# Expert weights with consecutive rows per partition, both output halves per down tile, and 32 copies of a relative bias

## The chip, the cores and the metric

The kernel runs on one core of a Trainium2 chip. The metric is the time of one execution on the device in microseconds, measured on the chip; the median of several executions counts.

## What is computed

A sequence of 256 tokens of width 1024 passes through two blocks of two layers each. A layer has a mixer (attention or a recurrence) and a mixture of experts (MoE) with 16 experts. All is float32. The change touches the MoE of the second block and, in its second layer, the reading of a relative bias that an attention mixer adds to its scores. Cut to that:

```python
D_MODEL, SEQ, DEPTH = 1024, 256, 2
MOE_EXPERTS, MOE_TOPK, MOE_FF = 16, 2, 512

def hier_moe(x, w_group, b_group, w_router, b_router, w_gate, w_up, w_down):
    t = x.reshape(-1, D)
    ...                                   # combine: weight of each expert for each token, two of 16 not zero
    y = jnp.zeros_like(t)
    for e in range(MOE_EXPERTS):          # w_gate[e], w_up[e]: (1024, 512); w_down[e]: (512, 1024)
        hdn = jax.nn.silu(t @ w_gate[e]) * (t @ w_up[e])
        y = y + combine[:, e:e + 1] * (hdn @ w_down[e])
    return y.reshape(B, S, D)

def second_block(x, ...):
    h = x
    for layer in range(DEPTH):
        if layer < N_A_LAYERS:
            mix = gla_mixer(h, ...)
        else:                             # scores get rel_table[rel_bucket(kpos - qpos)] as bias
            mix = diff_attention(h, ..., k1, k2, v, rel_table, lambda_init)
        h = layer_norm(DEEPNORM_ALPHA * h + mix, ln_g[layer, 0], ln_b[layer, 0])
        ffn = hier_moe(h, ..., moe_w_gate[layer], moe_w_up[layer], moe_w_down[layer])
        h = layer_norm(DEEPNORM_ALPHA * h + ffn, ln_g[layer, 1], ln_b[layer, 1])
        if layer == N_A_LAYERS - 1:
            k1, k2, v = shared_kv(h, kv_w)
    return h
```

In the first block the experts have an inner width of 256, in the second of 512.

## The kernel before

The four MoE layers are called moe10, moe11 (first block) and moe20, moe21 (second block); one function `moe` builds all of them. `F` is the inner width and `NF = F // 128` is 2 in the first block and 4 in the second. Tokens are gathered for the experts: every expert takes up to 64 tokens, and experts are worked on in eight **pairs** `pi`, so that the two experts of a pair fill the 128 columns of TensorE, expert `j` the columns `64 * j` and on. Two pairs make a group of four experts, for which `gather` fetches the tokens by matmuls with a one-hot matrix `oh` (tile `pg`, from `z` split in a high part `zh` and a low part `zl`).

For each pair there are these steps. `up(pi)` computes gate and up into two PSUM tiles `gu`, by 64 instructions over eight weight tiles of 1 MB, and takes silu of the gate part into `sa` (L794, ScalarE). `act(pi)` multiplies the up part, the combine weight `cr` and `sa` (L830, VectorE), and transposes the result by four matmuls into `pat` (L833), which VectorE copies back (L834). `down(pi)` multiplies by four down tiles of 1 MB: a tile is one half `h` of the output (512 of 1024 columns) and one half `fh` of the inner width, for both experts, and it is loaded by two DMAs of 512 KB, each of rows of 2 KB. When one half `h` of `y` is complete, ScalarE copies it rounded to `yh` (L860), VectorE makes the remainder `yl` (L861), and `spread` multiplies both by the one-hot matrix `st` to bring the rows back to their tokens (tile `sc`, recorded at L334, a helper for all split matmuls). `land` adds `sc` to the running `X` (L892, VectorE). Then the other half follows. `pst` (L820) is a transposition that makes `st`.

The loop runs `up(pi + 1)`, `down(pi)`, `act(pi + 1)` and so on; a scheduler orders the instructions of each engine. After pair 4 all engines read a counter and branch around an overflow path that does not run here (L905, L907). Weights come by `wload` and `fetch` on SP's queue (L193) into 19 slots in rotation; before the layer begins, a `plan` already loads the first 22 tiles. Gate and up tiles are read by `kview`: partition p gets row p, p + 128 and so on, four rows of 2 KB for each half of the 1024 rows. For this `z` stands in its natural order: chunk k of 128 columns is contraction step k.

The relative bias is prepared by `bias_task` while moe11's weights are already arriving. It writes the table `fsb` (8 heads, 384 values) 128 times over into a scratch array `fd` in HBM (L1542, on ScalarE's queue), so that partition p can later read its own copy shifted by p, with a row pitch of 383 (L1783, tile `vb`, two DMAs on ScalarE's queue, one for four heads each). `vb` is read there at the end of moe20, when its buffer comes free.

## Time and profile before

| | |
|---|---|
| median of 3 runs | 1602.59 us (1598.65 to 1603.44) |
| the profiled execution | 1602.16 us, of which the span is 1600.4 us |
| TensorE busy | 92% of the span |
| VectorE, ScalarE, GpSimd busy | 54%, 27%, 8% |
| mean DMA rate over the span | 288 GB/s |

A row of the timeline is a run of equal instructions on one engine: start and length in us, engine, line, operation, the tile written and those read, and in brackets the idle time ahead of it with what ended it. PE is TensorE, DVE is VectorE, ACT ScalarE, POOL GpSimd; "SPq" and "ACTq" are the queues of SP and ScalarE, from which DMAs are issued. One down or gate/up matmul of the program's order is two instructions in the profile.

### The profile page before, as it was taken

To read this page: it belongs to the slowest core of one execution; us is meant where nothing else is said; L and a number is where in the kernel's file an instruction comes from. 1 tells how busy PE (TensorE), PEld (TensorE's weight loads), DVE (VectorE), ACT (ScalarE), POOL (GpSimd) and SP (SyncE) were. 2 spreads that over 40 slices of the span, in tenths; PEclk is the share of its full clock that TensorE was granted. 3 is DMA by queue.
4 is the path that set the end of the run, shared out by engine and by line. 5 is a ranking of instruction groups with operands and counts; after the bars stand their busy time and mean duration, and the time that the engine had idled before them with its cause. 6 is when DMAs were issued, how large, how long until landed. Compare 5 with 4: busy or idle time off the path is not lost. (4 is left out here: it accounts for less than half of the span.)

```text
span 1600.4 us, 22811 instructions
## 1 busy us (share of the span) xinstructions
PE 1470.0 (92%) x9124; PEld 969.4 (61%) x9124; DVE 869.0 (54%) x1686; ACT 432.8 (27%) x733; POOL 129.2 (8%) x140
## 2 busy tenths in 40 slices
PE   4999987998889999889989999999998999999895
PEld 3879987443478999734448895443337988434331
DVE  3689998343678879823464574231127776212214
ACT  1454331211235434111125331110103652101000
POOL 0200002000121000300011001000003002000001
PEclk9999999999979999889999999999999999999998
DMA  9978799995855769799887487999999966999993
GB/s 301 365 249 273 259 303 324 353 302 198 268 174 173 242 232 337 167 363 359 292 263 214 133 290 267 386 387 353 381 334 288 298 195 244 341 386 387 346 386 124
DMA packets 324371, 461.69 MB, mean 288 GB/s; under 512 B 20077, under 2 KB 178285, under 8 KB 324258
## 3 DMA queue, kind: packets, MB, share of 16 engines
q1 hardware_dynamic: 308720, 446.34, 81.5%
q10 hardware_dynamic: 15538, 13.81, 3.5%
q8 instruction: 76, 1.25, 0.3%
q14 instruction: 37, 0.30, 0.1%
HBM read 456.43 MB, written 3.67 MB: 287 GB/s over the span
## 5 line engine op out<-in xcount | busy, mean ns | idle before, releaser
L786 PE MATMUL gu<-w,xg 128*64 128x512 f32 x1536 | 369.2, 597 | 0.0
L786 PEld LDWEIGHTS gu<-w,xg 128*64 128x64 f32 x1536 | 110.8, 137 | 209.1 <-issue 202.7
L356 DVE TENSOR_TENSOR wlo<-w,whi 128x2048 fp32r<-128x2048 f32 (+2 forms) x92 | 183.3, 1994 | 44.9 <-ACT whi L346 44.2
L850 PE MATMUL y<-w,sa 128*64 128x512 f32 x768 | 195.6, 607 | 4.4 <-DMA w<-in_w_exp_down_dram 4.4
L346 ACT ACTIVATE whi<-w 128x2048 fp32r<-128x2048 f32 (+2 forms) x92 | 157.9, 1726 | 151.4 <-PE acc L427 111.6
L850 PEld LDWEIGHTS y<-w,sa 128*64 128x64 f32 x768 | 55.0, 138 | 106.0 <-issue 97.7
L830 DVE SCALAR_TENSOR_TENSOR sa<-gu,cr,sa 128x256 f32<-128x256 f32 (+1 forms) x32 | 19.7, 615 | 163.6 <-PE gu L786 136.4
L334 PE MATMUL sc<-yy,st 128*128 128x512 f32 x256 | 88.8, 436 | 18.1 <-ACT yy L860 14.3
L522 DVE SCALAR_TENSOR_TENSOR adac<-w,ce,adac 128x512 f32<-128x512 f32 x140 | 104.7, 748 | 1.2
L427 PE MATMUL acc<-hl,whi 128*128 128x256 f32 x608 | 93.3, 286 | 0.0
L427 PE MATMUL acc<-hh,whi 128*128 128x256 f32 x608 | 90.4, 289 | 1.6 <-ACT whi L346 1.6
L892 DVE TENSOR_TENSOR x<-x,sc 128x512 f32<-128x512 f32 x112 | 74.3, 683 | 30.4 <-PE sc L334 30.3
L427 PE MATMUL acc<-hh,wlo 128*128 128x256 f32 x608 | 85.9, 281 | 0.0
L334 PE MATMUL pg<-oh,zh 128*128 128x256 f32 x256 | 73.8, 319 | 13.1 <-DVEq L907 7.3
L334 PEld LDWEIGHTS sc<-yy,st 128*128 128x128 f32 x256 | 42.0, 188 | 70.7 <-ACT yy L860 36.0
L427 PEld LDWEIGHTS acc<-hh,whi 128*128 128x128 f32 x608 | 78.4, 190 | 6.8 <-issue 4.1
L427 PE MATMUL acc<-whi,hh 128*128 128x256 f32 x416 | 70.9, 303 | 12.2 <-ACT hh L1240 8.9
L427 PEld LDWEIGHTS acc<-hl,whi 128*128 128x128 f32 x608 | 79.6, 189 | 3.7 <-issue 3.2
L427 PEld LDWEIGHTS acc<-hh,wlo 128*128 128x128 f32 x608 | 77.3, 188 | 1.0 <-issue 0.8
L334 PEld LDWEIGHTS pg<-oh,zh 128*128 128x128 f32 x256 | 55.4, 218 | 27.8 <-issue 15.0
L334 PE MATMUL pg<-oh,zl 128*128 128x256 f32 x256 | 71.2, 308 | 0.9 <-issue 0.9
L860 ACT ACTIVATE yy<-y 128x512 fp32r<-128x512 f32 x32 | 19.1, 597 | 192.2 <-PE y L850 192.2
(376 smaller groups left out, 2107.8 us busy)
## 6 DMA issues: line engine op xcount, KB each, us to landing
w<-in_moe_w_gate_dram SPq DMA_DIRECT2D x64, 1024.0 KB, 12.1
w<-in_moe_w_up_dram SPq DMA_DIRECT2D x64, 1024.0 KB, 13.8
w<-in_moe_w_down_dram SPq DMA_DIRECT2D x128, 512.0 KB, 11.6
w<-in_w_ada_dram SPq DMA_DIRECT2D x47, 1024.0 KB, 7.2
w<-in_w_in_dram SPq DMA_DIRECT2D x40, 1024.0 KB, 5.6
w<-in_w_exp_gate_dram SPq DMA_DIRECT2D x64, 512.0 KB, 9.5
w<-in_w_exp_up_dram SPq DMA_DIRECT2D x64, 512.0 KB, 8.8
w<-in_w_exp_down_dram SPq DMA_DIRECT2D x64, 512.0 KB, 8.9
```

Source lines behind the costliest of these rows:

```text
L334: PE.matmul(dst, l, r, start=(i == 0), stop=(i == n - 1), skip_group_check=True)
L346: S.activation(hi[:, k0:k0 + n], w, AF.Copy)
L356: eng.tensor_tensor(lo[:, k0 + x:k0 + y], w[:, x:y], hi[:, k0 + x:k0 + y].bitcast(F32), op=OP.subtract)
L427: PE.matmul(dst, l, r, start=(start and i == 0), stop=(i == n - 1), skip_group_check=True)
L522: V.scalar_tensor_tensor(acc, ws[k // 4][:, k % 4], ce[:, k:k + 1], acc, op0=OP.mult, op1=OP.add)
L786: PE.matmul(gu[64 * j:64 * j + 64, :], xg[:, 4 * kh + k, (2 * pr + j) * CAP:(2 * pr + j + 1) * CAP], ws[j][:, k, :], start=(kh == 0 and k ...
L830: V.scalar_tensor_tensor(sg, u, cr, sg, op0=OP.mult, op1=OP.mult)
L850: PE.matmul(y[64 * j:64 * j + 64, :], aT[:, f, 64 * j:64 * j + 64], w[:, j, k, :], start=(f == 0), stop=(f == NF - 1), tile_position=(0, 6 ...
L860: S.activation(yh[:, hs], src, AF.Copy)
L892: V.tensor_tensor(X[:, tt, hs], X[:, tt, hs], sc, op=OP.add)
```

## The change

The block-2 gate and up tiles are now read by `rview`: partition p gets the rows 8p to 8p + 7, of which a tile holds four, so 8 KB lie together in HBM. To match, `zh` and `zl` are written in the order (k c) from a source in the order (c k). The inner width is permuted in the same way: silu writes `sa` in the order (k c), the product in `act` reads the up part `u` from PSUM with a step of 16 bytes, and a down tile gives partition p the rows 4p to 4p + 3, of which it holds two, 8 KB together. A down tile now belongs to one expert `j` and one `fh`, holds both output halves, and is one DMA of 1 MB. Both halves of `y` are accumulated side by side, and they are copied and spread when all is done. `fd` has 32 copies; `vb` is read by eight DMAs of 32 partitions each, four for each half of the heads. The first block's MoE keeps its forms.

```diff
--- before.py
+++ after.py
@@ -117,6 +117,7 @@
 SM_TICKS = 4
 JOB_GAP = 2
 P_BUFS = 4
+FD = 32
 S_BANKS = 3
 DEC = 4
 TAGS = ("moe10", "moe11", "moe20", "moe21")
@@ -192,6 +193,10 @@
         for idx, src in parts:
             nc.sync.dma_start(w[idx] if idx is not None else w, src)
         return w
+
+    def rview(ap, n):
+
+        return ap.rearrange("(p k) n -> p k n", k=n)
 
     def kview(ap, c0, c1):
         return ap.rearrange("(k p) n -> p k n", p=P)[:, :, c0:c1]
@@ -674,11 +679,13 @@
                     mats = [[[((slice(None), slice(None), slice(i * 256, i * 256 + 256)), kview(w[e], 0, 256))
                               for i, w in enumerate((wg, wu))] for e in (ea, ea + 1)]]
                 else:
-                    mats = [[[(slice(None), kview(w[e], 0, 512))] for e in (ea, ea + 1)] for w in (wg, wu)]
+                    mats = [[[(slice(None), rview(w[e], KC))] for e in (ea, ea + 1)] for w in (wg, wu)]
                 return [([4, 512], [(idx, src[:, 4 * kh:4 * kh + 4]) for idx, src in mat[j]])
                         for mat in mats for kh in range(2) for j in range(2)]
 
             def down_tiles(pi):
+                if NF > 2:
+                    return [([2, D], [(None, rview(wd[2 * pi + j], NF)[:, 2 * fh:2 * fh + 2])]) for fh in range(2) for j in range(2)]
                 return [([2, 2, 512], [((slice(None), j), wd[2 * pi + j][fh * 256:(fh + 1) * 256, h * 512:(h + 1) * 512]
                                         .rearrange("(k p) n -> p k n", p=P)) for j in range(2)])
                         for h in range(2) for fh in range(NF // 2)]
@@ -791,7 +798,7 @@
                     if m == 0:
                         first = slots_of(pi, ow, oh) if NF > 2 else None
                         if NF > 2:
-                            S.activation(first[2], gu, AF.Silu)
+                            S.activation(first[2].rearrange("p (k c) -> p c k", k=NF), gu.rearrange("p (c k) -> p c k", k=NF), AF.Silu)
                 if NF == 2:
                     first = slots_of(pi, ow, oh)
                     S.activation(first[2], gus[0][:, 0:256], AF.Silu)
@@ -827,7 +834,11 @@
             def act(pi, st, cr, sg, u):
 
                 aT = both[0][:, pi % 2, 1].rearrange("p (f r) -> p f r", f=NF)
-                V.scalar_tensor_tensor(sg, u, cr, sg, op0=OP.mult, op1=OP.mult)
+                if NF == 2:
+                    V.scalar_tensor_tensor(sg, u, cr, sg, op0=OP.mult, op1=OP.mult)
+                else:
+                    sk = sg.rearrange("p (k c) -> p k c", k=NF)
+                    V.scalar_tensor_tensor(sk, u.rearrange("p (c k) -> p k c", k=NF), cr, sk, op0=OP.mult, op1=OP.mult)
                 pat = ps.tile([P, 512], F32, tag="tp", name="pat", bufs=2)
                 for f in range(NF):
                     PE.transpose(pat[:, f * P:(f + 1) * P], sg[:, f * P:(f + 1) * P], ident)
@@ -839,15 +850,28 @@
                 yy = mp.tile([P, 2, D], F32R, tag="yy", name="yy", bufs=1)
                 yh, yl = yy[:, 0], yy[:, 1]
                 yt = mp.tile([P, D], F32, tag="yt", name="yt", bufs=1) if gate is not None else None
-                for h in range(2):
-                    hs = slice(h * 512, (h + 1) * 512)
-                    y = ps.tile([P, 512], F32, tag=f"y{h}", name="y", bufs=1)
-                    for fh in range(NF // 2):
-                        w = wload(*todo[h * (NF // 2) + fh])
+                ypair = []
+                for fh in range(2 if NF > 2 else 0):
+                    ws = [wload(*todo[2 * fh + j]) for j in range(2)]
+                    for h in range(2):
+                        if fh == 0:
+                            ypair.append(ps.tile([P, 512], F32, tag=f"y{h}", name="y", bufs=1))
                         for k in range(2):
                             f = 2 * fh + k
                             for j in range(2):
-                                PE.matmul(y[64 * j:64 * j + 64, :], aT[:, f, 64 * j:64 * j + 64], w[:, j, k, :],
+                                PE.matmul(ypair[h][64 * j:64 * j + 64, :], aT[:, f, 64 * j:64 * j + 64],
+                                          ws[j][:, k, h * 512:(h + 1) * 512], start=(f == 0), stop=(f == NF - 1),
+                                          tile_position=(0, 64 * j), skip_group_check=True)
+                for h in range(2):
+                    hs = slice(h * 512, (h + 1) * 512)
+                    if NF > 2:
+                        y = ypair[h]
+                    else:
+                        y = ps.tile([P, 512], F32, tag=f"y{h}", name="y", bufs=1)
+                        w = wload(*todo[h])
+                        for f in range(2):
+                            for j in range(2):
+                                PE.matmul(y[64 * j:64 * j + 64, :], aT[:, f, 64 * j:64 * j + 64], w[:, j, f, :],
                                           start=(f == 0), stop=(f == NF - 1), tile_position=(0, 64 * j),
                                           skip_group_check=True)
                     if last and h == 1 and NF == 2:
@@ -928,7 +952,7 @@
                         for f in range(NF):
                             gw = mp.tile([P, 2, KC, P], F32, tag="yy", name="gw", bufs=1)
                             for i, w in enumerate((wg, wu)):
-                                S.dma_start(gw[:, i], kview(w[e], f * P, (f + 1) * P))
+                                S.dma_start(gw[:, i], (kview(w[e], 0, F) if NF == 2 else rview(w[e], KC))[:, :, f * P:(f + 1) * P])
                             pp = []
                             for i in range(2):
                                 q = ps.tile([P, 512], F32, tag="gu", name="q", bufs=2)
@@ -1049,13 +1073,23 @@
             V.scalar_tensor_tensor(t, cb[:, 0], mr[0], rp[tt][:, :n], op0=OP.mult, op1=OP.add)
             logits(tt, t, mr[1])
 
+        def parts_of(tt, src):
+
+            for h, hs in enumerate(halves):
+                if gate is not None:
+                    yield src[:, hs], z[0][:, tt, hs], z[1][:, tt, hs]
+                else:
+                    cs = slice(64 * h, 64 * h + 64)
+                    yield (src[:, hs].rearrange("t (c k) -> t c k", k=KC),
+                           *(y[:, tt].rearrange("t (k c) -> t c k", k=KC)[:, cs] for y in z))
+
         def high(tt, src):
-            for hs in halves:
-                S.activation(z[0][:, tt, hs], src[:, hs], AF.Copy)
+            for x, zh, _ in parts_of(tt, src):
+                S.activation(zh, x, AF.Copy)
 
         def low(tt, src):
-            for hs in halves:
-                G.tensor_tensor(z[1][:, tt, hs], src[:, hs], z[0][:, tt, hs].bitcast(F32), op=OP.subtract)
+            for x, zh, zl in parts_of(tt, src):
+                G.tensor_tensor(zl, x, zh.bitcast(F32), op=OP.subtract)
 
         def unit(tt, u):
             acc = ps.tile([P, 512], F32, tag="acc", name="acc", bufs=3)
@@ -1516,7 +1550,7 @@
 
 
     lam = cst.tile([P, 4], F32, name="lam")
-    fd = dram.tile([8, P, 384], F32, name="fd")
+    fd = dram.tile([8, FD, 384], F32, name="fd")
     fap = fd[:]
 
     def bias_task(ps, pool):
@@ -1539,7 +1573,7 @@
         yield 1
         fsb = pool.tile([8, 384], F32, tag="pT", name="fsb", bufs=3)
         V.tensor_copy(fsb, pf[0:8, :384])
-        S.dma_start(fd, fsb[:, None, :].to_broadcast([8, P, 384]))
+        S.dma_start(fd, fsb[:, None, :].to_broadcast([8, FD, 384]))
         yield 2
         t = pool.tile([P, 128], F32, tag="adas", name="ltm")
         tc.keep_in_program_order(V.tensor_tensor(t, ab[0], ab[1], op=OP.mult))
@@ -1780,8 +1814,9 @@
             v = [t[:, 0].rearrange("p (t n) -> p t n", t=2) for t in vb]
             Tb = [t[:, 1].rearrange("p (h n) -> p h n", h=4) for t in vb]
             for i in range(2):
-                S.dma_start(Tb[i], bass.AP(tensor=fap.tensor, offset=fap.offset + 127 + i * 4 * P * 384,
-                                           ap=[[383, P], [P * 384, 4], [1, 256]]))
+                for p0 in range(0, P, FD):
+                    S.dma_start(Tb[i][p0:p0 + FD], bass.AP(tensor=fap.tensor, offset=fap.offset + 127 - p0 + i * 4 * FD * 384,
+                                                           ap=[[383, FD], [FD * 384, 4], [1, 256]]))
             pbuf = slot(7, [4, 2, 256], "pbuf")
             pairs = [(0, 1), (2, 3)]
             gs = row_bcast(d, "gs", A["b_g_sub_2"][0])
```

On TensorE, at the end of moe20 (pairs 6 and 7), the order was, from the first down matmuls of pair 6 on; `y` is the down product, `pat` the transposition in `act`, `sc` the spreading:

```order
L850 MATMUL y<-w,sa 64x512 x4
L833 MATMUL pat<-consts,sa 128x128 x3
L850 MATMUL y<-w,sa 64x512
L833 MATMUL pat<-consts,sa 128x128
L850 MATMUL y<-w,sa 64x512 x4
L334 MATMUL sc<-yy,st 128x512 x4
L850 MATMUL y<-w,sa 64x512 x8
L334 MATMUL sc<-yy,st 128x512 x4
L850 MATMUL y<-w,sa 64x512 x7
L334 MATMUL sc<-yy,st 128x512 x4
L850 MATMUL y<-w,sa 64x512 x8
L334 MATMUL sc<-yy,st 128x512 x4
```

And with the change, at the same place:

```order
L862 MATMUL y<-w,sa 64x512 x2
L844 MATMUL pat<-consts,sa 128x128 x4
L862 MATMUL y<-w,sa 64x512 x14
L339 MATMUL sc<-yy,st 128x512 x4
L862 MATMUL y<-w,sa 64x512
L339 MATMUL sc<-yy,st 128x512 x4
L862 MATMUL y<-w,sa 64x512 x15
L339 MATMUL sc<-yy,st 128x512 x8
```

The 16 down matmuls of a pair stand together, only two of them ahead of the transposes, and the spreading of both halves follows behind all of them.

On ScalarE's queue, at the same place, the order around the bias copies `vb` was:

```order
L860 ACTIVATE yy<-y 128x512 x2
L1950 BRANCH_PREFETCH_HINT
L794 ACTIVATE sa<-gu 128x512
L1783 DMA vb<-fd 128x4x256 x2
L860 ACTIVATE yy<-y 128x512 x2
L233 DMA rows<-in_ln_g_dram 1x1024
```

And with the change:

```order
L884 ACTIVATE yy<-y 128x512 x2
L1985 BRANCH_PREFETCH_HINT
L801 ACTIVATE sa<-gu 128x128x4
L1818 DMA vb<-fd 32x4x256 x8
L884 ACTIVATE yy<-y 128x512 x2
L238 DMA rows<-in_ln_g_dram 1x1024
```

The copies stand at the same place, behind pair 7's silu and ahead of pair 6's copies of `y`, and are eight instead of two.

## Rows read from the trace of the kernel before

**Rows 1.** Page, part 1: busy time, share, instructions of each engine.
```profile
PE 1470.0 (92%) x9124; PEld 969.4 (61%) x9124; DVE 869.0 (54%) x1686; ACT 432.8 (27%) x733; POOL 129.2 (8%) x140
```

**Rows 2.** Stretches: length, busy PE, PEld, DVE, ACT, POOL, PEclk, DMA share, GB/s.
```profile
690.00:710.00 20.00, 15.60 (x53) 4.92 (x50) 2.76 (x7) 1.46 (x4) 1.23 (x2) 0.75 1.06 377
...
1000.00:1050.00 50.00, 50.00 (x236) 20.51 (x234) 13.26 (x22) 5.55 (x12) 1.18 (x2) 1.00 1.05 387
```

**Rows 3.** Page, part 5, spreading: busy, mean ns, idle before and its releaser.
```profile
L334 PE MATMUL sc<-yy,st 128*128 128x512 f32 x256 | 88.8, 436 | 18.1 <-ACT yy L860 14.3
```

**Rows 4.** Timeline, pair 4 of moe20, TensorE and VectorE's sa.
```profile
1118.84 1.89 PE L850 MATMUL y<-w,sa 128*64 128x512 f32 x8
...
1119.15 0.75 DVE L830 SCALAR_TENSOR_TENSOR sa<-gu,cr,sa 128x512 f32<-128x512 f32 x1 [12.60 <-PE gu L786]
...
1121.14 1.07 PE L850 MATMUL y<-w,sa 128*64 128x512 f32 x2
...
1125.02 0.49 PE L334 MATMUL sc<-yy,st 128*128 128x512 f32 x1 [0.68 <-ACT yy L860]
...
1125.74 0.95 PE L334 MATMUL sc<-yy,st 128*128 128x512 f32 x3 [0.23 <-DVE yy L861]
...
1126.62 3.65 PE L850 MATMUL y<-w,sa 128*64 128x512 f32 x14
...
1130.95 1.46 PE L334 MATMUL sc<-yy,st 128*128 128x512 f32 x4 [0.69 <-ACT yy L860]
...
1133.70 0.55 PE L334 MATMUL pg<-oh,zh 128*128 128x256 f32 x1 [1.29 <-DVEq L907]
```

**Rows 5.** TensorE's timeline at other late pairs of moe20 and moe21.
```profile
1091.33 1.89 PE L850 MATMUL y<-w,sa 128*64 128x512 f32 x8
...
1105.06 7.52 PE L786 MATMUL gu<-w,xg 128*64 128x512 f32 x34
...
1168.07 13.95 PE L786 MATMUL gu<-w,xg 128*64 128x512 f32 x64
1181.85 1.89 PE L850 MATMUL y<-w,sa 128*64 128x512 f32 x8
...
1561.44 1.89 PE L850 MATMUL y<-w,sa 128*64 128x512 f32 x8
...
1586.22 0.96 PE L334 MATMUL sc<-yy,st 128*128 128x512 f32 x3 [0.23 <-DVE yy L861]
```

**Rows 6.** TensorE's timeline in moe11.
```profile
701.33 1.94 PE L850 MATMUL y<-w,sa 128*64 128x512 f32 x2 [3.00 <-DMA w<-in_w_exp_down_dram]
704.67 6.37 PE L850 MATMUL y<-w,sa 128*64 128x512 f32 x14 [1.40 <-DMA w<-in_w_exp_down_dram]
```

**Rows 7.** DMA queue of ScalarE, 640 to 700 us: packets, MB, share of 16 engines.
```profile
q10 hardware_dynamic: 1032, 1.57, 21.1%
```

**Rows 8.** DMA queue of SP, 720 to 760 us, then 1000 to 1100 us.
```profile
q1 hardware_dynamic: 12223, 14.34, 107.7%
...
q1 hardware_dynamic: 19617, 38.59, 104.3%
```

**Rows 9.** SP's queue, timeline: DMA issues with their waits.
```profile
663.28 11.31 SPq L193 DMA_DIRECT2D w<-in_w_exp_up_dram  x1
...
1538.81 25.46 SPq L193 DMA_DIRECT2D w<-in_moe_w_down_dram  x16
```

**Rows 10.** SP's waits, 1150 to 1215 us: total, times, longest.
```profile
SPq L193 <- DMA vb<-fd: 13.4, 2, 10.3
```

**Rows 11.** ScalarE's queue, timeline at the end of moe20.
```profile
1178.63 3.79 ACTq L1783 DMA_DIRECT2D vb<-fd  x2
```

**Rows 12.** Page, part 6: KB each, median us from issue to landing.
```profile
w<-in_moe_w_down_dram SPq DMA_DIRECT2D x128, 512.0 KB, 11.6
```

**Rows 13.** GpSimd's timeline ahead of moe21.
```profile
1345.83 2.52 POOL L1058 TENSOR_TENSOR zl<-x,zh 128x512 fp32r<-128x512 f32 x2 [2.50 <-ACT zh L1054]
1351.48 1.30 POOL L769 TENSOR_TENSOR ow<-oh,r_c 128x256 f32<-128x256 f32 x2 [3.14 <-DVE oh L741]
```

## The prediction

> **What bounds the kernel now.** I read the shares of the engines first. TensorE is busy 1470.0 of 1600.4 us [rows 1], so the change can win only where TensorE stands or runs slowly, and can lose wherever it makes TensorE wait. The diff touches the two block-2 MoE layers (called moe20 and moe21 below) and one write of the relative bias, so next I read what TensorE does there. In the middle of moe20 it is busy 50.00 of 50 us while the DMA moves 387 GB/s [rows 2]: both are full, neither waits for the other. The idle time is elsewhere, in front of the spreading matmuls: the group "sc<-yy,st" stood idle 18.1 us, 14.3 of them behind ScalarE's copy yy at L860 [rows 3]. The timeline shows how. In a pair late in the layer TensorE finishes the eight matmuls (sixteen instructions) of one output half, stands 0.68 us until ScalarE has copied it, does one instruction, stands 0.23 us for VectorE's remainder, spreads, and does the same for the other half [rows 4]. In pairs 0 to 2 of a layer, gather and gate/up matmuls stand between and no such stop occurs; pairs 3 to 7 have it. There the pair's down part is bare.
>
> The second place is moe11, the block-1 layer in whose prefetch the fd write runs. [...]
>
> The run profiled took 1602.16 us (span 1600.4 us and 1.8 around it), 0.03% below the median 1602.59. All sums are against 1602.2. About 0.3% (4.8 us) is what a measurement here can tell from no change.
>
> **The fd write.** Before, 1024 rows of 1536 bytes went through a queue that took 21.1% of 16 engines over 60 us for 1032 packets [rows 7]: 0.211*16*60 = 203 us of engine time, 196 ns a packet. [...] With 32 copies there are 256 rows: 203 us becomes 51 us, and the disturbed stretch shrinks to a quarter. I take the two stops of 4.4 us as gone, because the tiles behind them were queued after the fd write. What is late next there is nothing: the activations these matmuls need are ready, since the stops are put down to the weights alone. The clock is the second part: after the stop 14 instructions take 6.37 us and two take 1.94 [rows 6], while in moe20 fourteen took 3.65 and two 1.07 [rows 4], so 2.7 + 0.9 = 3.6 us more. Together 4.4 to 8.0 us, chosen 7, as a little of it may come back as waits for weights further on.
>
> **The down tiles, pairs 3 to 7.** The order listed above the rows shows what the scheduler made of it: the two halves' matmuls run as one block of 16, of which 2 stand ahead of the four transposes "pat", and the spreading follows for both halves. Half 0 is complete four matmuls before half 1, 1.7 us, more than the 0.68, 0.49 and 0.23 in which the copy and the remainder come today [rows 4]. So the stops go. Content at full rate: 64 gate/up instructions take 13.95 us [rows 5], 0.215 each, so 32 down instructions take 6.9; the four transposes and the two of "pst" about 1.0; eight spreading ones 2.8.
> - Pair 3 takes 13.73 us from the end of gate/up to the next gate/up (1091.33 to 1105.06 [rows 5]). After: 6.9 + 1.0 + 2.8 + a new wait of 0.25 = 10.95. Gain 2.8. The new wait is for VectorE's product sa: it starts 0.3 us after gate/up ends and takes 0.75, and TensorE has only 0.86 us of down work ahead of the transposes now, where it had 1.89 [rows 4].
> - Pair 4 takes 14.86 us (1118.84 to 1133.70 [rows 4]), of which 1.29 is a wait for VectorE's queue at the overflow branch that stays. After: 10.7 + 0.25 + 1.3. Gain 2.6.
> - Pair 5 is built as pair 3, with a slightly longer way before: 2.9.
> - Pairs 6 and 7 stand behind each other with no gate/up left: 1561.44 to about 1587.1 in moe21 [rows 5], 25.6 us. After: 13.8 + 0.7 + 0.25 + 5.7 + 0.4 = 20.9, and 0.7 later at the end, since VectorE now has one more addition and its statistics behind the last spreading. Gain 4.0.
> - Pairs 0 to 2: the pat wait (+0.25) against one split down matmul less (1.07 us for two instructions in [rows 4], 0.43 at full rate): 0.
>
> Per layer 12.3 us, if the weights are there. In moe21 the last down tiles were issued until 1538.81 + 25.46 = 1564.3 us [rows 9] and such a tile lands 11.6 us after issue [rows 12], 1575.9; the last tile is used at about 1583, so 7 us to spare. TensorE gains 8.3 before pair 6 and comes that much closer; and a tile is now wanted for both halves at once, some 2 us sooner. I subtract 1.3: moe21 gains 11.
>
> In moe20 the end goes differently. **The bias copies**, now eight DMAs instead of two on ScalarE's queue, are issued at 1178.63 [rows 11], when gate/up of pair 7 sets their buffer free. In the built program every DMA of SP and ScalarE takes the next of eight completion semaphores and waits for the one that had it before. So SP stood 13.4 us behind vb in two waits [rows 10]. With eight such copies interleaved, the second two tiles of pair 6, one of pair 7 and the next phase's first load wait for a copy. Gate/up ends at 1181.85 [rows 5]; SP is let go about then, 2 MB and the copies take until about 7 us later (2 MB at 387 GB/s is 5.4), but TensorE wants them after 4.3 us, and the last tiles of pair 7, 4 MB further, some 19 us later. That is where the old order also ended (1181.85 + 25.6 = 1207.4). I therefore give moe20 nothing for pairs 6 and 7: 8 us in place of 12.3.
>
> **Rows of 8 KB.** Time per packet from the queue's share: with mostly 1 KB rows 1.077*16*40/12223 = 56 ns for 1173 bytes, with 2 KB rows 1.043*16*100/19617 = 85 ns for 1967 bytes [rows 8]. That is 0.0365 ns a byte and 13 ns fixed. An estimate for 8 KB is 312 ns, against 352 for four of 2 KB: at most 11% less; at the least nothing. No row of 8 KB data is in this trace, so a loss is not excluded either. I take 4%, a third, and book it at nothing: it shifts weights, not TensorE, and only has to keep them ahead of the faster TensorE. [...]
>
> **The order of z, silu and u.** z is written by ScalarE and, at 2.52 us for two instructions, by GpSimd, which ends at 1348.35 and then idles 3.14 us until VectorE's oh, for which the gather matmuls wait too [rows 13]. Half as slow again would add 1.3 us there: covered. Silu runs under the up matmuls. On the path is only sa at L830, which now reads PSUM 16 bytes apart. Bounds: unchanged 0.75, or doubled 1.5; less is excluded, as nothing about the sum it computes gets smaller. I take unchanged.
>
> Sum: 1602.2 - 7 - 8 - 11 = **1576**.
>
> **Rivals.**
> - *Strided sa.* If L830 takes 1.5 us, every pair's transposes come 0.75 later, with nothing between: 16 * 0.75 = 12, 1588. [...] For it speaks that nothing covers this wait; against it that only one of the three operands is strided. Chance 0.14.
> - *The copies chain further.* The eight copies hold SP longer than I take it, TensorE stands 7 us in moe20's last pairs and the next phase: 1583. For it: 13.4 us of waits are there already. Chance 0.16.
> - *No gain in the late pairs.* The stops only change their name into waits for weights, and the fd write alone stays: 1595. Against it: 7 us to spare. It would show as idle time before "y" and "gu" behind DMA. Chance 0.07, within 0.3% in half the cases.
> - *Slower: 8 KB rows stream worse.* A layer's 96 MB take 260 us at 387 GB/s. At 4% less the stream ends 10 us later per layer, 7 of them spare, which eats the 7 of the fd write: that is the point from which it is a loss. At 6% it is 15.6 - 7 = 8.6 a layer, 17 - 7 = 10 in all: 1612, the late pairs' gains gone since TensorE waits. For it: the shape has no row here, and the DMA is full in [rows 2]. Against it: time per byte falls from 1 KB to 2 KB rows. Chance 0.10.
>
> **How the numbers follow.** The forecast, 1576, has 0.53; the first two rivals 0.30 and stay faster by more than 4.8 us; the third 0.07, half of it within 0.3%; the slower one 0.10, three parts of it beyond 4.8 us. Faster 0.85, same 0.06, slower 0.09. The range: downwards the fd term at 8, moe20's pairs 6 and 7 at 4.0 and moe21 at 12.3 give 1570, and 8 KB rows that shorten later waits some more: 1563. Upwards to the third rival: 1597. About 0.15 is left out.
>
> **What would show it.** Right: the fd write's queue at a quarter of its share; no idle time before "y" around 700 us; "sc" with almost no wait for L860; 8 KB packets under 340 ns; pairs 6 and 7 of moe21 in 21 us. Wrong: L830 above 1 us and idle time before "pat"; idle time before "y" or "gu" behind DMA; SP's waits for vb well above 13.4 us; a rate under 387 GB/s in the middle of a layer.

## The result, and the profile after

The changed kernel takes 1586.35 us (1584.6 to 1587.22), the kernel before on the same chip 1603.01. The ratio is 0.9898, with a 95% interval of 0.9876 to 0.9921: faster by 16.7 us where 26 were forecast. The time lies in the range of 1563 to 1597. The profiled execution took 1586.74 us, with a span of 1584.9; all comparisons of stages below are between its span and the 1600.4 us of before, one execution each.

First the page: the shares of the engines, and from its part 5 (busy time, mean ns of one, idle before) the down matmuls of block 2, the spreading and the product sa.

```profile
PE 1465.2 (92%) x9124; PEld 971.0 (61%) x9124; DVE 864.1 (55%) x1686; ACT 443.1 (28%) x733; POOL 131.1 (8%) x140
...
L862 PE MATMUL y<-w,sa 128*64 128x512 f32 x512 | 132.6, 596 | 3.3 <-DMA w<-in_moe_w_down_dram 3.3
...
L339 PE MATMUL sc<-yy,st 128*128 128x512 f32 x256 | 83.9, 429 | 6.0 <-DVE yy L885 3.2
...
L841 DVE SCALAR_TENSOR_TENSOR sa<-gu,cr,sa 128x512 f32<-128x512 f32 x16 | 12.0, 751 | 125.6 <-PE gu L793 125.6
```

The stops ahead of the spreading are gone: 6.0 us instead of 18.1 [rows 3]. The product sa, which now reads PSUM 16 bytes apart, takes 0.751 us, as before [rows 4]. But TensorE's busy time fell by 4.8 us only [rows 1], and the down matmuls have a new wait for weights.

Next the stretches of [rows 2], with the same columns (length, busy PE, PEld, DVE, ACT, POOL, PEclk, DMA share, GB/s):

```profile
690.00:710.00 20.00, 20.00 (x106) 10.15 (x102) 8.63 (x16) 4.35 (x9) 1.23 (x2) 1.00 1.07 368
1000.00:1050.00 50.00, 50.00 (x238) 20.65 (x236) 12.56 (x21) 6.49 (x12) 1.18 (x2) 1.00 1.01 420
```

Around 700 us TensorE no longer stands, and its granted clock is 1.00 where it was 0.75. In the middle of moe20 the DMA moves 420 GB/s instead of 387, with TensorE as full as before. The queues over 640 to 700 us (ScalarE's) and 1000 to 1100 us (SP's), packets, MB and share:

```profile
q10 hardware_dynamic: 536, 1.44, 8.6%
...
q1 hardware_dynamic: 5608, 40.80, 98.3%
```

A weight packet now carries 7275 bytes and takes 0.983*16*100/5608 = 280 ns. The timeline of TensorE in moe11, which answers [rows 6], shows no stop:

```profile
695.44 3.65 PE L874 MATMUL y<-w,sa 128*64 128x512 f32 x16
699.02 0.44 PE L844 MATMUL pat<-consts,sa 128*128 128x128 f32 x2
```

Now the late pairs. This is pair 3 of moe20, which answers the first two rows of [rows 5]:

```profile
1079.90 1.88 PE L862 MATMUL y<-w,sa 128*64 128x512 f32 x4
1081.71 0.66 PE L844 MATMUL pat<-consts,sa 128*128 128x128 f32 x4
1082.20 0.38 PE L827 MATMUL pst<-consts,ow 128*128 128x128 f32 x2
1082.51 7.08 PE L862 MATMUL y<-w,sa 128*64 128x512 f32 x28
1089.53 1.20 PE L339 MATMUL sc<-yy,st 128*128 128x512 f32 x4
1090.65 1.07 PE L793 MATMUL gu<-w,xg 128*64 128x512 f32 x2
1091.69 1.25 PE L339 MATMUL sc<-yy,st 128*128 128x512 f32 x4
1092.87 13.52 PE L793 MATMUL gu<-w,xg 128*64 128x512 f32 x61
```

No row has a bracket: nothing stands. Yet from the start of the down part to the second run of gate/up it is 12.97 us, where 10.95 were forecast. Four down instructions take 1.88 us, 0.47 each, and 28 take 7.08, 0.25 each, where 0.215 were counted. In the order of the built program the experts of the 16 down matmuls read 0 0, then the transposes, then 1 0 1 1 0 1 0 0 1 0 1 1 0 1. Before it was 0 1 0 1 0 1 0 1 for each half of the output, with transposes between. In the program matmuls of different experts use different halves of TensorE's columns, matmuls of one expert the same half (`tile_position=(0, 64 * j)`). Two stretches inside the run of 28 show what that does (length, busy PE with the number of instructions, PEclk, DMA share, GB/s):

```profile
1082.50:1087.28 4.78, 4.77 (x22) 1.00 1.01 420
1087.94:1089.53 1.59, 1.59 (x4) 1.00 1.02 423
```

In the first stretch the instructions start in twos, 0.43 us from two to two, although an expert follows itself three times in these 14 matmuls. The last four instructions, like the four ahead of the transposes, start one by one, again 0.43 us apart. So what counts is not the direct neighbour: the 14 hold eight matmuls of expert 1 and six of expert 0, so two are left without a partner, and so are the two of expert 0 that stand ahead of the transposes. These four lone matmuls, eight instructions, cost 8 * 0.215 = 1.7 us more than in twos, an estimate from these two rates. That is most of what is missing: the 32 instructions take 1.88 + 7.08 = 8.96 us, not 6.9. A lone matmul also stands in the spreading now (gate/up x2, 1.07 us).

Last the end of moe20, pairs 6 and 7, with SP's wait for the bias copies from 1130 to 1205 us (total, times, longest):

```profile
1168.18 3.65 PE L862 MATMUL y<-w,sa 128*64 128x512 f32 x12
1172.46 1.93 PE L862 MATMUL y<-w,sa 128*64 128x512 f32 x4 [0.63 <-DMA w<-in_moe_w_down_dram]
1176.52 3.65 PE L862 MATMUL y<-w,sa 128*64 128x512 f32 x12 [2.13 <-DMA w<-in_moe_w_down_dram]
...
1187.65 3.65 PE L862 MATMUL y<-w,sa 128*64 128x512 f32 x14 [0.57 <-DMA w<-in_moe_w_down_dram]
...
1194.86 3.61 PE L1021 MATMUL warm<-consts 128*128 128x256 f32 x16
...
SPq L194 <- DMA vb<-fd: 34.0, 4, 24.9
```

TensorE stands 3.33 us for down weights, and four instructions behind the first stop take 1.93 us. SP waited 34.0 us behind vb, against 13.4 [rows 10].

Where the 15.5 us of the two spans lie, by the start or end of TensorE's rows at four places (us, after minus before; forecast on the right):

| stage | after | forecast |
|---|---|---|
| start to the first gather of moe20 | -11.4 | -7 |
| from there to the end of gate/up of pair 7 | -3.9 | -8.3 |
| from there to the first gather of moe21 | +5.6 | 0 |
| moe21 to the end | -5.8 | -11 |

In the first line 2.8 of the 11.4 were already there at the first transposes of moe11, which start 15.7 us after the first gather of that layer, where the profile of before takes 18.4: its first 3.6 us there ran at a granted clock of 0.50, those of the changed kernel at 1.00. That is not the change, for the kernels below with the down tiles alone and with the gate/up rows alone, which write 128 copies, take 15.7 too, and the one with all but the copies takes 18.4. But with 128 copies the head start is mostly lost again: those two then stand 6.8 and 6.9 us for down weights, where before stands 4.4. From the first transposes to those of the next pair it is 19.1 us before, 20.3, 20.3 and 19.3 in these three, and 10.0 in the changed kernel. So the write itself is worth 8.6 to 10.3, according to which kernel is compared.

### The profile page after: what moved, and what is told of

Its sections match the earlier page's. It is cut to its first block, busy times and chain, and to the rows that moved or that the text cites. A ratio compares the mean times of both kernels' runs of the same rounds, so it can differ in the third digit from the quotient of the medians.

```text
span 1584.9 us, 22763 instructions
## 1 busy us (share of the span) xinstructions
PE 1465.2 (92%) x9124; PEld 971.0 (61%) x9124; DVE 864.1 (55%) x1686; ACT 443.1 (28%) x733; POOL 131.1 (8%) x140
## 5 line engine op out<-in xcount | busy, mean ns | idle before, releaser
L862 PE MATMUL y<-w,sa 128*64 128x512 f32 x512 | 132.6, 596 | 3.3 <-DMA w<-in_moe_w_down_dram 3.3
L862 PEld LDWEIGHTS y<-w,sa 128*64 128x64 f32 x512 | 43.1, 137 | 80.3 <-issue 72.5
L339 PE MATMUL sc<-yy,st 128*128 128x512 f32 x256 | 83.9, 429 | 6.0 <-DVE yy L885 3.2
L916 DVE TENSOR_TENSOR x<-x,sc 128x512 f32<-128x512 f32 x112 | 74.3, 682 | 24.1 <-PE sc L339 24.1
L841 DVE SCALAR_TENSOR_TENSOR sa<-gu,cr,sa 128x512 f32<-128x512 f32 x16 | 12.0, 751 | 125.6 <-PE gu L793 125.6
L829 DVE TENSOR_SCALAR st<-pst 128x256 fp32r<-128x256 f32 x24 | 10.2, 423 | 121.7 <-ACT pst L828 121.7
L885 DVE TENSOR_TENSOR yy<-y,yy 128x512 fp32r<-128x512 f32 x32 | 22.0, 688 | 97.0 <-ACT yy L884 97.0
```

What stands on the lines that cost most here:

```text
L339: PE.matmul(dst, l, r, start=(i == 0), stop=(i == n - 1), skip_group_check=True)
L829: V.tensor_scalar(st, pst[:, :T], 0.0, None, op0=OP.is_gt)
L841: V.scalar_tensor_tensor(sk, u.rearrange("p (c k) -> p k c", k=NF), cr, sk, op0=OP.mult, op1=OP.mult)
L862: PE.matmul(ypair[h][64 * j:64 * j + 64, :], aT[:, f, 64 * j:64 * j + 64], ws[j][:, k, h * 512:(h + 1) * 512], start=(f == 0), stop=(f == ...
L885: V.tensor_tensor(yl[:, hs], src, yh[:, hs].bitcast(F32), op=OP.subtract)
L916: V.tensor_tensor(X[:, tt, hs], X[:, tt, hs], sc, op=OP.add)
```

## The experiments

All ratios are to the kernel before, run on the same chip. The medians come from several chips, so where two kernels lie close it is the ratios that compare them.

### The parts by themselves

Three kernels do one part each: the copies, with their eight reads; the gate/up rows with the order of z (`parts_of`, `high` and `low` as in the change); the down tiles with the order of silu and u. A fourth does all but the copies.

```diff
# e2_copies_alone, against before
+FD = 32
-    fd = dram.tile([8, P, 384], F32, name="fd")
+    fd = dram.tile([8, FD, 384], F32, name="fd")
...
# e3_gate_up_rows_alone, against before
-kview(w[e], 0, 512)
+rview(w[e], KC)
...
# e4_down_tiles_alone, against after
-FD = 32
+FD = 128
-rview(w[e], KC)
+kview(w[e], 0, 512)
-                if gate is not None:
+                if True:
...
# e11_all_but_the_copies, against after
-FD = 32
+FD = 128
```

> The kernel before with 32 copies of the bias and eight reading DMAs, nothing else. Prediction: 7 us, 1596. The trace of the changed kernel has moe20 begin 11.4 us earlier, and nothing but the copies changed ahead of that: 1591 to 1593, less what the eight reads cost at the end of moe20 (up to 3). If only the two stops of 4.4 us count: 1598.

> The kernel before with gate and up weights of block 2 in rows of 8 KB and z in that order; down tiles, silu and bias copies as before. Theory: TensorE sets the pace, so no difference, 1600 to 1605, with a DMA rate above 387 GB/s in the middle of the layers. Rival: the strided writes of z delay the first gather, 1604 to 1608. Rival: faster weights shorten waits, 1598 or less.

> The kernel before with the new down tiles and the silu order, z and gate/up rows and 128 bias copies as before. By the prediction's terms 8 + 11 = 19 us: 1584. By theory A of the first run, with the order of the experts not pinned here either: 12.3 less five times 1.9 for each layer, about 3 each, 1596 to 1599.

> The changed kernel with 128 copies of the bias and two reads, as before: rows, order and down tiles of the change stay. Alone the copies gave 11.5 us, the down tiles 16.9 and the gate/up rows -1.4, together 27, while the whole change gave 16.7. If the copies are worth 11.5 here too, 1598 us, and rows and down tiles hinder each other. If the down tiles keep their 17 with the rows, 1586 to 1588, and it is the copies that give nothing on top: then moe11 must still end some 10 us earlier in the changed kernel, and the loss must lie between the end of moe20 and moe21, where the eight reads are.

| kernel | median us | ratio, 95% interval |
|---|---|---|
| copies alone | 1591.99 | 0.9938 [0.9917, 0.9959] |
| gate/up rows alone | 1604.91 | 1.0007 [0.9991, 1.0023] |
| down tiles alone | 1586.66 | 0.9895 [0.9864, 0.9926] |
| all but the copies | 1591.00 | 0.9935 [0.9921, 0.9948] |

By the ratios (times 1603) the copies alone gain 9.9 us, the gate/up rows lose 1.1, the down tiles gain 16.8, all but the copies gain 10.4, and all together 16.4. So with the rest in place the copies gain about 5 (6.0 by the ratios, 4.7 by the medians 1591.00 and 1586.35). In moe11 the stops come back with 128 copies, here in the kernel with all but the copies:

```profile
701.41 1.94 PE L874 MATMUL y<-w,sa 128*64 128x512 f32 x2 [3.13 <-DMA w<-in_w_exp_down_dram]
704.92 6.25 PE L874 MATMUL y<-w,sa 128*64 128x512 f32 x14 [1.58 <-DMA w<-in_w_exp_down_dram]
```

The transposes of two successive pairs stand 19.3 us apart around them, 10.0 in the changed kernel: 9.3 us for the write. What is lost again lies at the end of moe20. With two reads of vb this kernel has no stop there, and it takes 22.5 us from the end of gate/up (1176.29 + 0.59) to the row "warm":

```profile
1178.38 7.08 PE L862 MATMUL y<-w,sa 128*64 128x512 f32 x28
...
1199.36 3.62 PE L1021 MATMUL warm<-consts 128*128 128x256 f32 x16
```

Before it was 25.4, and in the changed kernel it is 28.2. So the down tiles gain 2.9 there and the eight reads take 5.7.

Gate/up rows of 8 KB are worth nothing that can be measured, although their packets raise the rate to 399 GB/s in the middle of moe20 and to 420 with the down tiles. Their 1604.91 us lie in the range of the theory and in that of its rival, a delay of the first gather by the strided writes of z; that delay is in the trace (below, "Strided operands").

Of the other three, the copies alone came where their expectation had them. The down tiles alone came near the 1584 of the prediction's terms and far from the 1596 to 1599 of theory A (of the next part), which took the loss by the order too high for them. All but the copies, at 1591.00, lies between its two expectations.

The parts do not add up: 9.9 - 1.1 + 16.8 = 25.6, and all together give 9.2 less. Some 2 us of the gap are the reads: from the end of gate/up of pair 7 to the first gather of moe21 they cost 4.4 us when the copies stand alone (15.0 ahead of before there, 10.6 at the gather) and 6.3 in the full change (below, +5.6 against -0.7). Some 5 lie between the sum of gate/up rows and down tiles, 15.7, and the two together, 10.4, although the profiled executions of down tiles alone and of all but the copies differ by 1.0 us of span only (1587.8 and 1588.8); that of the down tiles alone was the longest of its four (1589.57 us, median 1586.66). Gathers run at either clock from one execution to the next (the instructions of "pg" start 0.12 or 0.21 us apart, some 1.5 us a gather), which blurs such differences. This part is not settled.

### Order on TensorE

```diff
# e1_pairs_in_order, against after
+            fourth = []
...
-                for f in range(NF):
-                    PE.transpose(...)
+                with tc.issue_after(fourth[0]) if fourth else ExitStack():
+                    for f in range(NF):
+                        PE.transpose(...)
...
-                                PE.matmul(ypair[h]...)
+                                mm = PE.matmul(ypair[h]...)
+                                if (f, h, j) != (0, 0, 0):
+                                    tc.keep_in_program_order(mm)
+                                if (f, h, j) == (1, 0, 1):
+                                    fourth[:] = [mm.ins]
```

> The changed kernel with one thing pinned: the 16 down matmuls of a pair keep the written order, in which the two experts alternate, and the transposes come behind at least the fourth of them. Theory A: the changed kernel lost its gain because the scheduler put two matmuls of the same expert behind each other (first two and last two of each late pair run alone, 0.43 us an instruction instead of 0.215): about 1.9 us back in each of the five late pairs of both layers, 19 us at most; in moe20 the weights behind the bias copies stop part of it, so 1567 to 1577 us. Theory B, the late pairs are held by weights whatever the order: waits behind DMA take the place, 1583 to 1588.

It took 1580.86 us, ratio 0.9855 [0.9823, 0.9888]: 6.9 us below the changed kernel by the ratios, whose intervals still touch, and between the two theories. The experts now alternate, eight matmuls ahead of the transposes and eight behind. Pair 3 of moe20 takes 12.45 us instead of 12.97, and not 10.95: one matmul of expert 0 stands alone between the two transpositions pst, which leaves one of expert 1 without a partner behind them, and a gate/up matmul still stands alone in the spreading (each lone one takes 1.07 us for its two instructions).

Two more kernels go on from there. The first adds the move of the reads (next section) to this one; the second also puts pst behind what stands on TensorE, and holds the first gate/up matmul and pair 7's first down matmul in the program's order.

```diff
# e9_no_matmul_alone, against e6_pairs_in_order_reads_behind
+                                if NF > 2 and pi > 4 and (m, kh, k, j) == (0, 0, 0, 0):
+                                    tc.keep_in_program_order(mm)
...
-                    for tt in range(2):
-                        PE.transpose(pst[:, tt * P:(tt + 1) * P], pair(ow, tt), ident)
+                    with after_last(ENG.PE) if NF > 2 and pi > 3 else ExitStack():
+                        for tt in range(2):
+                            PE.transpose(pst[:, tt * P:(tt + 1) * P], pair(ow, tt), ident)
...
-                                if (f, h, j) != (0, 0, 0):
+                                if (f, h, j) != (0, 0, 0) or pi == 7:
```

> Both edits together: the down matmuls in the written order and the reads behind the weights. If the two are independent: 1586.35 - 5.5 - 5 = 1576 us. If the faster TensorE of moe20 runs into weights that come too late whatever the reads do: 1580, with idle time before y or gu behind DMA.

> As the sixth run (down matmuls in the written order, reads behind the weights), and besides the transposes pst stay in the middle of gate/up and the next pair's first gate/up or down matmul stays behind the spreading, so that no matmul of one expert stands alone between others in the late pairs. If two matmuls of different experts run side by side only when they stand together, each alone one costs 0.43 us and its two switches some more: pairs 3 and 5 should take 10.5 to 11 us beside gate/up (12.45 in the first run, 12.97 in the changed kernel), about 1.5 less each, and pairs 6 and 7 0.6 less: 7 us in both layers, 1569 us. If that is not the cause: 1576 as before. If weights become the limit: in between, with idle time before y or gu behind DMA.

They took 1576.24 us, 0.9837 [0.9813, 0.9861], and 1572.72 us, 0.9825 [0.9804, 0.9847]. The first meets its forecast of 1576. It is also the cleanest comparison for the order of experts: with the reads behind the weights and the order left, the ratio is 0.9892 [0.9868, 0.9916] (next section), so the intervals are apart and the order is worth 8.8 us. The second was forecast at 1569; over the first it gains 1.9 us by the ratios, whose intervals overlap, though its profiled execution is 5.7 us shorter. It has the lowest time of all. Its pair 3:

```profile
1078.69 3.60 PE L867 MATMUL y<-w,sa 128*64 128x512 f32 x16
1082.22 0.66 PE L849 MATMUL pat<-consts,sa 128*128 128x128 f32 x4
1082.81 3.65 PE L867 MATMUL y<-w,sa 128*64 128x512 f32 x16
1086.39 1.19 PE L339 MATMUL sc<-yy,st 128*128 128x512 f32 x4
1087.99 1.84 PE L339 MATMUL sc<-yy,st 128*128 128x512 f32 x4 [0.41 <-DVE x L925]
1089.76 7.09 PE L793 MATMUL gu<-w,xg 128*64 128x512 f32 x32
```

That is 11.07 us where 10.95 were forecast, but with pst (0.38 us in the changed kernel) now inside gate/up; 16 instructions take 3.60 us, 0.225 each. The same 512 down instructions of block 2 in three kernels whose down matmuls wait for nothing, from the page: the reads moved and the order left, the order of experts mended, no matmul alone.

```profile
L862 PE MATMUL y<-w,sa 128*64 128x512 f32 x512 | 130.2, 595 | 0.0
```
```profile
L864 PE MATMUL y<-w,sa 128*64 128x512 f32 x512 | 124.2, 595 | 0.0
```
```profile
L867 PE MATMUL y<-w,sa 128*64 128x512 f32 x512 | 114.4, 594 | 0.0
```

With the same instructions and the same mean of one, order alone is worth 15.8 us of this line's busy time, 7.9 a layer; of TensorE's whole busy time 11.1 are left (1464.8 to 1453.7). The mean cannot show it: it is the time from an instruction's start to its end, and two that run side by side each have it in full (512 of 595 ns are 305 us, in 114.4 to 130.2 us of busy time). The busy sum shows it.

### Where the reads of vb stand

```diff
# e5_reads_behind_weights, against after (e7: the same, against e2)
-                    S.dma_start(Tb[i][p0:p0 + FD], ...)
+                    with after_last(ENG.SP):
+                        nc.sync.dma_start(Tb[i][p0:p0 + FD], ...)
...
# e10_no_matmul_alone_reads_on_gpsimd, against e9
-                    with after_last(ENG.SP):
-                        nc.sync.dma_start(Tb[i][p0:p0 + FD], ...)
+                    G.dma_start(Tb[i][p0:p0 + FD], ...)
```

> The changed kernel with the eight reads of the bias copies issued on SP's queue, behind all down tiles of moe20 and two loads of the next phase, instead of on ScalarE's queue. Theory C: the reads hold SP through shared completion semaphores (34.0 us of waits in four) and so cost moe20's pairs 6 and 7 their weights: these waits of 3.3 us go, and moe20 ends 4 to 6 us sooner, 1580 to 1582 us. Rival: the tail is bound by the DMA's rate anyway, 1585 to 1588.

> The kernel before with 32 copies and the reads on SP's queue behind the weights; nothing else. Separates the write of the copies from the reading: if the reads cost 4.5 us in the second run (copies alone, 1592.0), 1587 to 1588; if not, 1592 again.

> As the ninth run, but with the eight reads issued by GpSimd, whose DMAs use other completion semaphores than those of SP and ScalarE and stand in no weight's way. The reads on SP's queue delayed the next phase's weights (SP waited 10.9 us between two of them), and the projection behind moe20 lost about 3 us by it: if so 2 to 4 us less than the ninth run; if the projection's weights come at the DMA's rate anyway, the same.

On SP's queue behind the weights: 1584.46 us, 0.9892 [0.9868, 0.9916], for the change, which is 1586.35 without it; 1589.13 us, 0.9926 [0.9899, 0.9953], for the copies alone, 1591.99 without. By the ratios that is 1.0 and 1.9 us, with intervals that overlap: neither gain is clear of noise; the first missed its forecast of 4 to 6 us, and the second lies between its two. Yet the mechanism is there. The end of moe20 has no stop and takes 22.5 us again, 5.7 less; with the copies alone it takes 25.4 instead of 29.3. The gain is lost in the next projection, which takes 36.0 us where the changed kernel takes 32.6: SP now stands behind a load on ScalarE's queue (SP's waits from 1130 to 1215 us), the DMA moves nothing in the 15 us behind "warm" (0 GB/s, 295 in the changed kernel), and TensorE waits for the split of a weight:

```profile
SPq L194 <- DMA rows<-in_ln_g_dram: 24.0, 1, 24.0
...
1218.55 1.22 PE L432 MATMUL acc<-hh,wlo 128*128 128x256 f32 x8 [2.30 <-DVE wlo L361]
```

On GpSimd's queue all of the gain went: 1599.60 us, 0.9995 [0.9979, 1.001], 27 us above the kernel with no matmul alone, which neither expectation allowed for. Two rows of GpSimd's timeline, and TensorE's longest wait, in the layer norm behind moe20:

```profile
1158.66 0.88 POOL L1828 DMA_DIRECT2D vb<-fd  x1 [39.60 <-DMA w<-in_moe_w_down_dram]
1165.34 0.57 POOL L1828 DMA_DIRECT2D vb<-fd  x1 [5.80 <-issue]
```
```profile
PE pt L326 <- DVE x L307: 31.7, 1, 31.7
```

GpSimd issued the first six of the eight reads 6.3 to 7.2 us apart. The layer norm's rs runs on GpSimd too; it stood behind them, VectorE's x waits for it, and TensorE 31.7 us for x. Which completion semaphores GpSimd's DMAs use no row here shows.

### Row length of the down tiles

```diff
# e8_down_rows_4k, against after
-rview(wd[2 * pi + j], NF)[:, 2 * fh:2 * fh + 2]
+kview(wd[2 * pi + j], 0, D)[:, 2 * fh:2 * fh + 2]
...
-S.activation(first[2].rearrange("p (k c) -> p c k", k=NF), gu.rearrange("p (c k) -> p c k", k=NF), AF.Silu)
+S.activation(first[2], gu, AF.Silu)
```

> The changed kernel with down rows of 4 KB instead of 8 (each partition gets two rows 128 apart), hence silu and the product in the natural order, everything else as changed. Theory: the gain of the down tiles is the two halves being accumulated together, not the length of the rows, and the strided silu costs nothing: 1584 to 1588, as the changed kernel. Rival: the rows matter, since the late pairs live on the DMA's lead: 1590 or more, with waits for down weights. Rival: the strided operations cost, 1583 or less.

It took 1584.66 us, 0.9892 [0.9869, 0.9915], as the changed kernel. Rows of 4 KB with silu and u in natural order do as well; the middle of moe20 runs at 417 GB/s. So neither 8 KB down rows nor the permuted inner width cost or gain anything here that the intervals could show.

## Why the prediction was right and wrong

The forecast was right in sign, and its mechanisms appeared; it missed 10 us. By the stages below, the late pairs of both layers gave 9.6 us less than their terms, one term of the sum being mis-sized; the end of moe20 cost 2.8 and the stage behind it 2.9, both booked at nothing. Ahead of moe20 4.4 more came in than forecast. Some of that, up to 2.8, is luck: the clock of moe11's gathers in the two executions profiled.

**The fd write: right, a little too small.** Forecast 7, measured 8.6 to 10.3, according to the kernel that is compared. Both parts came: the two stops of 3.00 and 1.40 us [rows 6] and the slow clock behind them, 0.75 over 690 to 710 us [rows 2], are gone. The queue's share did not fall to a quarter as listed, but only to 8.6%, since the load of `x`, 1.05 MB, now lies in this stretch (1.44 MB, of which the write is 0.39).

**The late pairs: the mechanism right, the content mis-sized.** The stops went as foretold, and the pat wait is small. The step that failed is "32 down instructions take 6.9": they took 8.96. It took the rate of 64 gate/up instructions, in which the experts alternate, for down matmuls whose order of experts was never read. The order of the built program was on the table as counts ("y x2, pat x4, y x14"), which do not show the expert. In pair 3 of moe20 the gain was 0.8 where 2.8 were forecast; pairs 6 and 7 of moe21 took 22.7 us from the end of gate/up, against 25.6 before and 20.9 forecast; and moe21 as a whole gave 5.8 instead of 11. The kernel with no matmul alone shows what the term is worth at full rate, though it also mends lone gate/up matmuls. By stages (us against before):

| stage | forecast | after | all but the copies | experts in order | no matmul alone, reads behind |
|---|---|---|---|---|---|
| to the first gather of moe20 | -7 | -11.4 | +0.5 | -11.6 | -12.6 |
| to the end of gate/up of pair 7 | -8.3 | -3.9 | -5.6 | -6.0 | -9.2 |
| to the first gather of moe21 | 0 | +5.6 | -0.7 | +4.6 | +0.4 |
| moe21 to the end | -11 | -5.8 | -5.8 | -7.7 | -10.1 |

The last column meets the forecast in the two stages of the late pairs to 0.9 us, less than the clock of one gather moves (some 1.5 us). The rival "no gain in the late pairs" named another cause, waits for weights; of its sign, idle time before "y" behind DMA, there is nothing in moe21 and the 3.3 us in moe20's end.

A part of pair 4's wait had not been counted: the two halves of sc now come so close that TensorE waits 0.97 us for VectorE's addition at L916, to have a PSUM tile free, ahead of the 1.14 us for VectorE's queue at the overflow branch, which stayed as said.

```profile
1117.50 1.24 PE L339 MATMUL sc<-yy,st 128*128 128x512 f32 x4 [0.97 <-DVE x L916]
```

**The bias copies: right in kind, the price too low.** That SP would stand behind vb and that pairs 6 and 7 of moe20 would win nothing was forecast. SP's waits rose from 13.4 to 34.0 us, TensorE stood 3.3 us, and the end of moe20 became 2.8 us longer instead of equal; the layer norm, mixer and routing behind it lost 2.9 more, which has other causes (below). It is the rival "the copies chain further", whose price was 7, and the experiments bear it out in kind: with two reads, or with the eight behind the weights, the stops are gone and the tail is 5.7 us shorter. That moving the reads then won next to nothing in time is the projection's loss, told above.

**The stage behind moe20: booked at nothing, and it lost 2.3 us in the kernel with all but the copies, 2.9 in the changed one and 4.3 in the one with no matmul alone.** It has two parts. The larger lies in the projection: from its first matmul to the first of the mixer it takes 30.7 us before, 32.6 in the changed kernel and 34.1 in the one with no matmul alone. The profile has 18 us of it at a lower granted clock. In order: before, after, and the 15 and 18 us behind "warm" of the kernel with no matmul alone (columns as in [rows 2]).

```profile
1222.00:1240.00 18.00, 18.00 (x153) 17.86 (x152) 11.10 (x12) 8.47 (x8) 2.44 (x2) 1.00 0.99 264
```
```profile
1209.40:1227.40 18.00, 17.81 (x139) 17.61 (x138) 9.28 (x10) 8.51 (x8) 2.47 (x2) 0.92 1.10 283
```
```profile
1181.30:1196.30 15.00, 11.57 (x55) 9.34 (x54) 14.49 (x20) 2.41 (x3) 9.06 (x6) 0.80 0.00 0
1196.30:1214.30 18.00, 17.43 (x129) 17.21 (x129) 8.68 (x9) 7.20 (x7) 2.50 (x2) 0.88 0.92 237
```

By estimate 18 us at a granted clock of 0.92 are 1.4 us lost, most of the 1.9. In the last kernel the 18 us at 0.88 make 2.2 of the 3.4; in the 15 us ahead the clock was 0.80 and the DMA moved nothing, as with the reads moved alone. Not all of this belongs to the change: with the copies alone and with the gate/up rows alone the projection takes 1.4 us longer than before as well, and of all the kernels only the one with the reads on GpSimd has it as short (30.3). TensorE comes there from a spell with idle time in all of them, before included; why the clock held in the profile of before, and whether it does in its other executions, is not settled. The smaller part, 0.7 us right ahead of moe21's first gather, does belong to the change (below, "Strided operands").

**Rows of 8 KB: right that the time does not move.** The rate rose by 8.5%, to 420 GB/s, more than the 4% taken and near the estimate of 11%, since 280 ns a packet of 7275 bytes is just what the prediction's estimate of 13 ns and 0.0365 ns a byte gives (279). The rival with slower rows fell. The runs with 4 KB down rows (1584.66 us) and with gate/up rows alone (1604.91 us) show that faster weights bought nothing here where TensorE is the bound, busy 50.00 of 50 us.

**Strided operands: the rival fell, but z was not covered.** VectorE's product took 751 ns, unchanged. ScalarE's silu and zh, which now write their elements 512 bytes apart, became nearly twice as long (busy us, mean ns, idle before; 597 and 632 ns before):

```profile
L801 ACT ACTIVATE sa<-gu 128x512 f32<-128x512 f32 x8 | 8.6, 1072 | 69.4 <-PE gu L793 69.4
...
L1088 ACT ACTIVATE zh<-x 128x512 fp32r<-128x512 f32 x4 | 4.1, 1127 | 7.0 <-DVE x L1055 7.0
```

Why ScalarE's strided writes slowed and VectorE's strided read did not, no run shows. Silu was covered, as booked. The order of z was not, and this step failed in small: "half as slow again would add 1.3 us there: covered" looked at GpSimd, which does end ahead of oh, and not at VectorE beside it. VectorE's comparisons for the routing, `k_gt`, take long when GpSimd's zl runs beside them (1.10 to 1.62 us for 128x128, against 0.29 us), and TensorE waits for their result `r_m` at `pos`, just ahead of the gathers. Here they are ahead of moe21, with TensorE's waits for both layers (total, times, longest), before and after:

```profile
1345.93 1.21 DVE L546 TENSOR_TENSOR k_gt<-k_gt,consts 128x32 f32<-128x32 f32 x1
...
1347.39 1.10 DVE L544 TENSOR_TENSOR k_gt<-el 128x128 f32<-128x128 f32 x1
...
1348.53 0.29 DVE L546 TENSOR_TENSOR k_gt<-k_gt,consts 128x128 f32<-128x128 f32 x1
...
PE pos L725 <- DVE r_m L558: 1.7, 2, 1.0
```
```profile
1335.52 0.18 DVE L551 TENSOR_TENSOR k_gt<-k_gt,consts 128x32 f32<-128x32 f32 x1
...
1335.91 3.05 POOL L1092 TENSOR_TENSOR zl<-x,zh 128x512 fp32r<-128x512 f32 x2 [3.00 <-ACT zh L1088]
...
1335.96 1.62 DVE L549 TENSOR_TENSOR k_gt<-el 128x128 f32<-128x128 f32 x1
...
1337.61 1.49 DVE L551 TENSOR_TENSOR k_gt<-k_gt,consts 128x128 f32<-128x128 f32 x1
...
PE pos L732 <- DVE r_m L563: 2.8, 2, 1.4
```

zl takes 3.05 us where it took 2.52 [rows 13], and it now runs beside both comparisons of 128x128, where one of them came behind it in 0.29 us. The three together take 3.29 us instead of 2.60, which are the 0.7 us. All nine kernels with the new order of z wait 2.8 us at `pos`; the four with the old one wait 1.4 or 1.7. So the order of z costs 1.1 to 1.4 us, about what the gate/up rows alone lose by the ratio, though that loss by itself lies within the noise.

## What to carry to other kernels

Where two matmuls are to share TensorE by columns, count partners, not instructions (here 16 instructions took 3.60 us in twos, and 4 without partners 1.88): read from the built order which half each one uses, see whether both halves get equally many between two instructions that use all columns, and pin the order if a scheduler may choose. A stop removed from a full engine is worth its length only if the work behind it keeps its rate (here the idle time ahead of the spreading fell by 12.1 us, and pair 3 of moe20 gained 0.8 of the 2.8 us forecast); check that by the busy sum of a line, not by the mean of one instruction. A transfer split in eight, on a queue whose transfers the weights' queue waits for (SP stood 34.0 us behind vb, 13.4 with two), can cost more than the larger transfer it replaces (5.7 us here), and it is best costed at the place where it is read. An instruction that became slower is covered only if those beside it keep their length too (zl took 3.05 us instead of 2.52, and the comparisons beside it 3.29 instead of 2.60).

## What the runs showed of the hardware

- Matmuls of 64 columns: 0.22 us an instruction when those of the two column halves run in twos (16 in 3.60 us), 0.47 when one half has no partner (4 in 1.88 us), with a mean of 594 to 596 ns over the 512 of each kernel. They need not be direct neighbours: in a block of 14 matmuls, eight on one half and six on the other, 24 of the 28 instructions started in twos although three times a half followed itself.
- The granted clock of one and the same stretch (18 us of the projection behind moe20, after 15 us in which TensorE was busy 10.4, 10.4 and 11.6 us) was 1.00, 0.92 and 0.88 in the profiles of three kernels whose instructions there are of the same kinds.
- In the middle of moe20 (1000 to 1050 us) the core's DMA moved 420 GB/s with rows of 8 KB, 417 with down rows of 4 KB, 387 with 2 KB.
- ScalarE slowed from 597 to 1072 ns when it wrote its elements 512 bytes apart; VectorE reading PSUM 16 bytes apart did not (751 ns before and after).
- A VectorE comparison of 128x128 took 0.29 us with no GpSimd instruction beside it and 1.10 to 1.62 us beside GpSimd's zl; one of 128x32 took 0.18 and 1.21.
- The first six of eight DMAs issued by GpSimd went out 6.3 to 7.2 us apart and held up its arithmetic; TensorE stood 31.7 us in the end.
